# Two of four weight-quarter sums of a Strassen-type up projection: from VectorE to GpSimd

## The chip, the cores and the metric

The kernel runs on one core of one Trainium2 chip. The metric is the device time of one execution in microseconds; the figure given for a kernel is the median of its runs.

## What is computed

One layer of a hybrid encoder on 512 tokens of 2048 channels, all in float32: a normalised input projection, a convolution branch and a neighbourhood attention branch, an output projection, and then the part that matters here, a gated MLP with 5632 hidden units:

```python
xn = rms_norm(x, ffn_norm_g[l])
up = jnp.einsum("bsd,df->bsf", xn, w_up[l])          # 2048 -> 2 * 5632
up = depthwise_conv(up, ffn_dw_w[l], ffn_dw_b[l])    # width 3
gate, val = jnp.split(up, 2, axis=-1)
x = x + jnp.einsum("bsf,fd->bsd", jax.nn.silu(gate) * val, w_down[l])
return rms_norm(x, final_norm_g)
```

## The kernel before

Every matrix is split into a high part (float32 rounded to the format that TensorE multiplies in one pass) and a low part (the rest). A product is then three matmuls, `hi*mh`, `hi*ml` and `lo*mh` (lines 120, 121 and 122). Weights arrive in units of 128 x 1024 float32 (512 KB). A unit is loaded by the SP queue (line 104, tile `raw`), ScalarE copies its high part (line 109, `whi`), VectorE subtracts to get the low part (line 110, `wlo`), and TensorE uses both for 24 matmuls.

All units stand in one list, `plan`, in the order in which TensorE uses them. `weights()` is called ahead of each product and makes units until three beyond the present one exist (`AHEAD = 3`). `whi` and `wlo` have four buffers each, `raw` seven; the sums of weights (`ws`) take theirs from the same seven. A scheduler lays out each engine's instructions in a fixed order at build time, by priority and by its own estimate of when operands are ready; at run time each engine and each queue works through its order strictly.

The up projection goes tile by tile over 44 tiles `f` of 128 hidden units; a tile has a gate half and a value half, and the reduction over 2048 channels is cut in two as well. That makes a 2 x 2 scheme of weight quarters A11, A21, A22, A12, each 128 x 1024, and of token halves of 256 columns, and instead of eight products the kernel makes seven (c = 0 to 6), in the manner of Strassen and Winograd. The factors of the seven products are made by `factors(f)`: three are quarters as they are (c = 0, 3, 5), four are sums:

- c = 1, line 539: `ws = A21 + A22`
- c = 2, line 541: `A21 = A21 + A11`, in place in the tile of A21
- c = 4, line 546: `ws = ws + A11`
- c = 6, line 550: `ws = ws + A12`

Each is one instruction on tiles of 128 x 1024, and `add` is `nc.vector.tensor_add`. The sum then goes through the same two steps as any unit (lines 109 and 110). The results of the seven products (`pu`, three accumulators in turn for c = 0 to 5 and another one for c = 6) are put together on ScalarE and VectorE: the copies `vv` and `uu` (lines 602 and 606) and the adds of lines 605 to 611. Then come the scaling by the norm (627, 628), the convolution (619 on ScalarE, 620 and 621 on VectorE), the Silu (630) and the product with the value half (631).

Four tiles make a group, and there are eleven groups. At the end of a group its four results are split into `hh` (line 636, ScalarE) and `hl` (line 637, VectorE). The down projection of a group runs during the next group, one unit of `w_down` behind the products c = 3 and c = 6 of each tile (line 120 to 122 with `pd`). Its results are copied by ScalarE (line 649, `pdc`) and added to the residual in DRAM by accumulating transfers that GpSimd issues (line 650, `x2d<-pdc`); apart from a few small instructions at the start that is all that GpSimd does. The first group has no down projection beside it, and in the last group the units are spread otherwise. The last group's own down projection comes at the end, with the final norm.

Of the kernel before, what the change touches and what calls it, by code (L numbers as in the profile page):

```python
# [13 lines left out]
ALU = mybir.AluOpType  # L14
# [50 lines left out]
def layer(ctx: ExitStack, tc: tile.TileContext, xT, w_in, w_out, w_up, w_down, par, tab, out):  # L65
    nc = tc.nc
# [19 lines left out]
    def t4(shape, name):  # L86

        return wpool.tile(shape, F32, tag="raw", name=name, bufs=NR)
# [13 lines left out]
    def raw_unit(src, n):  # L102
        raw = t4([P, U * P], "raw")
        return raw, nc.sync.dma_start(raw[:, :n], src)

    def parts(raw, n):
        hi = wpool.tile([P, U * P], F32R, tag="whi", name="whi", bufs=NW)
        lo = wpool.tile([P, U * P], F32R, tag="wlo", name="wlo", bufs=NW)
        i = nc.scalar.activation(hi[:, :n], raw[:, :n], AF.Copy)  # L109
        j = nc.vector.tensor_sub(lo[:, :n], raw[:, :n], hi[:, :n].bitcast(F32))  # L110
        return hi, lo, i, j
# [416 lines left out]
    def factors(f):  # L528

        def load(q):  # L530
            a[q] = raw_unit(w_up[f, q], U * P)[0]
            return a[q]

        def make(c):
            if c == 0:
                return load(A22)
            if c == 1:
                a["s"] = t4([P, U * P], "ws")
                add(a["s"], load(A21), a[A22])
            elif c == 2:  # L540
                add(a[A21], a[A21], load(A11))
                return a[A21]
            elif c == 3:
                return a[A11]
            elif c == 4:
                add(a["s"], a["s"], a[A11])
            elif c == 5:
                return load(A12)
            else:
                add(a["s"], a["s"], a[A12])  # L550
            return a["s"]

        a = {}
        return [lambda c=c: parts(make(c), U * P)[:2] for c in range(7)]

    A11, A21, A22, A12 = range(4)
    add = nc.vector.tensor_add
# [203 lines left out]
```

## Time and profile before

| | us |
|---|---|
| median of 3 runs | 2101.67 |
| lowest and highest run | 2101.33, 2106.94 |
| profiled execution, span from the first to the last instruction | 2106.4 |
| TensorE busy in it | 2067.0 |
| VectorE busy | 1575.8 |
| ScalarE busy | 988.8 |
| GpSimd busy | 140.1 |

The page of the profile gives the span of the profiled execution and no other time of it. In its rows PE is TensorE, PEld its weight loads, DVE VectorE, ACT ScalarE, POOL GpSimd and SP the queue that issues most transfers. A group's row names the line, the engine, the operation, what is written from what, the shapes, the count, then the busy time and the mean of one, and after the bar how long the engine stood idle ahead of these instructions and what ended that. A row of a timeline gives start and length in us, then the instruction, and in brackets the idle time ahead of it and what ended it. A row of waits gives who waited for whom, the total, the number of times and the longest.

### The profile page before, as it was taken

How to read it: one execution, taken by the hardware profiler on the slowest of the kernel's cores; microseconds unless marked ns; L12 is line 12 of the kernel's file. 1: busy time of each engine (PE TensorE's matmuls, PEld its weight loads, DVE VectorE, ACT ScalarE, POOL GpSimd, SP SyncE). 2: the span in 40 equal slices, each digit the busy share in tenths (PEclk: the TensorE clock that was granted, in tenths of full speed). 3: DMA queues.
4: the chain of work that ended last, by engine and by line, in shares of the span. 5: the costliest groups of instructions: out<-in, count | busy, mean ns of one | idle time of the engine just before them, and what ended most of it. 6: DMA issues, size and time to landing. Idle time of an engine off the chain costs nothing.

```text
span 2106.4 us, 32366 instructions
## 1 busy us (share of the span) xinstructions
PE 2067.0 (98%) x13024; PEld 1853.7 (88%) x13024; DVE 1575.8 (75%) x2137; ACT 988.8 (47%) x1472; POOL 140.1 (7%) x166
## 2 busy tenths in 40 slices
PE   8999999999999999999999999999999999999997
PEld 6888888877878899999999999999999999998986
DVE  7986796686568897777777777777776777768666
ACT  6144424456436554454544544454454445444442
POOL 0000000000000001110111101101001011010110
PEclk9999999999999999999999999999999999999998
DMA  6233223236224235565565555556656556553672
GB/s 226 90 121 100 92 89 105 99 108 213 97 96 135 80 121 135 127 138 141 122 142 138 135 136 141 130 131 145 138 127 141 141 131 131 140 135 99 145 203 81
DMA packets 95910, 270.89 MB, mean 129 GB/s; under 512 B 10640, under 2 KB 14736, under 8 KB 95760
## 3 DMA queue, kind: packets, MB, share of 16 engines
q1 hardware_dynamic: 72720, 226.88, 34.4%
q0 software_dynamic: 23040, 41.95, 14.4%
q8 instruction: 102, 1.67, 0.3%
q14 instruction: 48, 0.39, 0.1%
HBM read 218.46 MB, written 50.33 MB: 128 GB/s over the span
## 4 chain that ended last, share of the span: by engine, by line
PE 96%; DVE 2%; DMA 1%; ACT 1%; issue 0%; SPq 0%; DVEq 0%; ACTq 0%
PE pu L120 14%; PE pu L122 14%; PE pu L121 14%; PE pd L122 8%; PE pd L120 8%; PE pd L121 8%; PE pj L120 7%; PE pj L122 7%; PE pj L121 7%; PE po L120 3%; PE po L121 3%; PE po L122 3%; PE sc L366 1%; PE po L409 1%; PE trp L396 1%; DMA raw<-in_w_up 1%
## 5 line engine op out<-in xcount | busy, mean ns | idle before, releaser
L110 DVE TENSOR_TENSOR wlo<-raw,whi 128x1024 fp32r<-128x1024 f32 x368 | 449.3, 1222 | 361.8 <-ACT whi L109 336.6
L120 PE MATMUL pu<-xc,whi 128*128 128x256 f32 x2464 | 699.8, 284 | 8.2 <-ACT vv L602 4.7
L122 PE MATMUL pu<-xc,wlo 128*128 128x256 f32 x2464 | 699.5, 284 | 0.0
L121 PE MATMUL pu<-xc,whi 128*128 128x256 f32 x2464 | 699.5, 284 | 0.0
L109 ACT ACTIVATE whi<-raw 128x1024 fp32r<-128x1024 f32 x368 | 389.2, 1059 | 627.7 <-PE pj L121 217.1
L120 PEld LDWEIGHTS pu<-xc,whi 128*128 128x128 f32 x2464 | 474.5, 193 | 12.8 <-ACT vv L602 4.9
L121 PEld LDWEIGHTS pu<-xc,whi 128*128 128x128 f32 x2464 | 474.6, 193 | 3.5 <-issue 0.4
L122 PEld LDWEIGHTS pu<-xc,wlo 128*128 128x128 f32 x2464 | 474.5, 193 | 0.0
L650 POOL DMA_DIRECT2D x2d<-pdc x160 | 139.4, 873 | 1902.0 <-ACT pdc L649 1794.1
L120 PE MATMUL pj<-xh,whi 128*128 128x512 f32 x640 | 254.0, 398 | 7.7 <-ACT whi L109 7.7
L120 PE MATMUL pd<-hh,whi 128*128 128x512 f32 x640 | 250.3, 391 | 1.9 <-ACT pdc L649 1.9
L122 PE MATMUL pj<-xh,wlo 128*128 128x512 f32 x640 | 250.6, 392 | 0.7 <-DVE wlo L110 0.6
L121 PE MATMUL pj<-xl,whi 128*128 128x512 f32 x640 | 251.2, 393 | 0.0
L121 PE MATMUL pd<-hl,whi 128*128 128x512 f32 x640 | 250.3, 391 | 0.0
L122 PE MATMUL pd<-hh,wlo 128*128 128x512 f32 x640 | 248.9, 391 | 0.0
L109 ACT ACTIVATE whi<-ws 128x1024 fp32r<-128x1024 f32 x132 | 139.9, 1060 | 192.9 <-PE pu L121 135.1
L280 DVE SCALAR_TENSOR_TENSOR y<-ch,prm,y 128x507 f32<-128x507 f32 (+14 forms) x240 | 170.1, 741 | 3.1
L110 DVE TENSOR_TENSOR wlo<-ws,whi 128x1024 fp32r<-128x1024 f32 x132 | 161.3, 1222 | 12.4 <-ACT whi L109 11.8
L649 ACT ACTIVATE pdc<-pd 128x512 f32<-128x512 f32 x160 | 94.0, 588 | 133.4 <-PE pd L122 133.3
L120 PEld LDWEIGHTS pj<-xh,whi 128*128 128x128 f32 x640 | 120.8, 189 | 36.1 <-ACT whi L109 9.0
L122 PEld LDWEIGHTS pj<-xh,wlo 128*128 128x128 f32 x640 | 120.7, 189 | 27.7 <-DVE wlo L110 2.1
L122 PEld LDWEIGHTS pd<-hh,wlo 128*128 128x128 f32 x640 | 120.3, 188 | 28.1 <-DVE wlo L110 3.4
(141 smaller groups left out, 2452.7 us busy)
## 6 DMA issues: line engine op xcount, KB each, us to landing
raw<-in_w_up SPq DMA_DIRECT2D x176, 512.0 KB, 3.5
raw<-in_w_down SPq DMA_DIRECT2D x88, 512.0 KB, 4.0
raw<-in_w_in SPq DMA_DIRECT2D x80, 512.0 KB, 3.7
x2d<-pdc POOLq DMA_DIRECT2D x160, 256.0 KB, 4.7
raw<-in_w_out SPq DMA_DIRECT2D x32, 512.0 KB, 3.4
x<-in_xT SPq DMA_DIRECT2D x32, 256.0 KB, 6.0
tab<-in_tab SPq DMA_DIRECT2D x32, 256.0 KB, 4.0
x2d<-x SPq DMA_DIRECT2D x16, 256.0 KB, 2.0
```

What stands on the lines that cost most here:

```text
L109: i = nc.scalar.activation(hi[:, :n], raw[:, :n], AF.Copy)
L110: j = nc.vector.tensor_sub(lo[:, :n], raw[:, :n], hi[:, :n].bitcast(F32))
L120: nc.tensor.matmul(ps, hi[:, a], mh, start=start, stop=False)
L121: nc.tensor.matmul(ps, hi[:, a], ml, start=False, stop=False)
L122: return nc.tensor.matmul(ps, lo[:, a], mh, start=False, stop=stop)
L280: nc.vector.scalar_tensor_tensor(y[:, a:b], h[:, a + j - PAD:b + j - PAD], prm[:, o + j:o + j + 1], y[:, a:b], op0=ALU.mult, op1=ALU.add)
L366: m = nc.tensor.matmul(both[:, j, i, :], q[hp, b * P:(b + 1) * P], grid(k, KC0[b], KW)[hp], start=True, stop=True)
L396: m = nc.tensor.transpose(ps[:, 2 * i + ch, :], s[:, i, ch * P:(ch + 1) * P], ident)
L409: m = nc.tensor.matmul(grid(po, b * BLK, BLK)[hp], vt[b // 2][:, 2 * (b % 2) + ch, hp], pts[j][:, 2 * i + ch, :], start=(ch == 0), stop=(c ...
L649: nc.scalar.activation(t, ps, AF.Copy)
L650: nc.gpsimd.dma_start(xd[d], t, accum_op=ALU.add)
```

## The change

The sums for c = 1 and c = 2 are issued on GpSimd; those for c = 4 and c = 6 stay on VectorE. Operands, order in the program, tiles and everything else are as before.

```diff
             if c == 1:
                 a["s"] = t4([P, U * P], "ws")
-                add(a["s"], load(A21), a[A22])
+                nc.gpsimd.tensor_tensor(a["s"], load(A21), a[A22], op=ALU.add)
             elif c == 2:
-                add(a[A21], a[A21], load(A11))
+                nc.gpsimd.tensor_tensor(a[A21], a[A21], load(A11), op=ALU.add)
                 return a[A21]
```

## The prediction

> **What bounds the kernel now.** I read the page's first part, then the table of windows, then the waits of TensorE in the gated MLP, and last the rows around each wait. A window row gives the stretch, its length, then busy time and count for PE, PEld, DVE, ACT and POOL, and the granted clock.
>
> ```profile
> PE 2067.0 (98%) x13024; PEld 1853.7 (88%) x13024; DVE 1575.8 (75%) x2137; ACT 988.8 (47%) x1472; POOL 140.1 (7%) x166
> ```
>
> ```profile
> 740.27:760.43 20.16, 20.16 (x170) 20.16 (x169) 20.11 (x25) 10.05 (x13) 0.00 (x0) 1.00 0.33 111
> ...
> 1200.00:1500.00 300.00, 300.00 (x2078) 280.62 (x2078) 221.44 (x260) 142.54 (x188) 33.05 (x38) 1.00 0.59 137
> ```
>
> TensorE is the bound: it is busy for all of the 300 us of the second window at full clock, and nothing that only makes VectorE lighter there can show. VectorE is busy 74% of it. The first window is one tile of hidden units in the first group of four, where no down-projection units are interleaved: there VectorE is busy 20.11 of 20.16 us, so both engines are full at once. The kernel can therefore win only where TensorE waits, and lose wherever VectorE is already just in time. TensorE's waits from the end of the output projection on, and those of its weight loads, are few:
>
> ```profile
> PE pu L120 <- ACT vv L602: 4.7, 1, 4.7
> PE pu L120 <- ACT whi L109: 3.5, 1, 3.5
> ```
>
> ```profile
> PEld pd L122 <- DVE wlo L110: 3.4, 8, 0.4
> ```
>
> The first is one wait of 4.7 us, the second one of 3.5 us at the start of the MLP. The third is the telling one: eight times the weight load of a down product waits up to 0.4 us for VectorE's low half. Eight times VectorE has no slack left at all.
>
> **What moves, and its price.** The two adds of L539 and L541 run 44 times each on VectorE:
>
> ```profile
> L541 DVE TENSOR_TENSOR raw<-raw 128x1024 f32<-128x1024 f32 x44 | 53.7, 1221 | 4.7 <-DMA raw<-in_w_up 4.7
> ...
> L539 DVE TENSOR_TENSOR ws<-raw 128x1024 f32<-128x1024 f32 x44 | 53.6, 1219 | 3.1 <-DMA raw<-in_w_up 3.1
> ```
>
> ```profile
> L650 POOL DMA_DIRECT2D x2d<-pdc x160 | 139.4, 873 | 1902.0 <-ACT pdc L649 1794.1 <-ACT uu L606 95.2 <-DMA raw<-in_w_down 12.7
> masks.py:199 POOL TENSOR_SCALAR_AFFINE_SELECT ident<-ident 128x128 f32<-128x128 f32 x1 | 0.3, 287 | 0.1
> masks.py:197 POOL MEMSET ident<- 128x128 f32 x1 | 0.2, 204 | 0.3 <-POOLq L753 0.3
> L753 POOL MEMSET const-bfloat16-1.0<- 128x1 bf16 x1 | 0.1, 101 | 0.0
> ```
>
> The rows around one of them, in the timelines of VectorE and GpSimd at a boundary between two groups:
>
> ```profile
> 911.76 1.23 DVE L110 TENSOR_TENSOR wlo<-raw,whi 128x1024 fp32r<-128x1024 f32 x1 [3.56 <-ACT whi L109]
> 912.95 0.75 DVE L620 SCALAR_TENSOR_TENSOR uy<-g,prm,uy 128x511 f32<-128x511 f32 x1
> 913.62 1.22 DVE L539 TENSOR_TENSOR ws<-raw 128x1024 f32<-128x1024 f32 x1
> 914.75 0.75 DVE L621 SCALAR_TENSOR_TENSOR uy<-g,prm,uy 128x511 f32<-128x511 f32 x1
> ...
> 919.14 1.22 DVE L110 TENSOR_TENSOR wlo<-raw,whi 128x1024 fp32r<-128x1024 f32 x1
> ```
>
> ```profile
> 912.62 0.87 POOL L650 DMA_DIRECT2D x2d<-pdc  x1 [2.58 <-ACT pdc L649]
> ```
>
> One add lasts 1.22 us on VectorE and holds its queue for 1.13 us (913.62 to 914.75). On GpSimd no add is shown. The nearest rows: 128 columns written take 204 ns and one column 101, so a written column is 0.81 ns; one input more makes it 287 ns, so a column read is about 0.65 ns. An add of 1024 columns that reads two inputs and writes one is estimated at 0.1 + 1024 x (0.81 + 2 x 0.65) ns = 2.26, say 2.3 us. The bounds are VectorE's own 1.22 us below, and above twice a one-input pass, 2 x (0.1 + 1024 x 1.46 ns) = 3.2 us. GpSimd's total becomes 140 + 88 x 2.3 = 342 us, far from full. Its queue is in order: an add may stand behind an issue of L650 that waits for the copy of a down product, and an issue behind an add that waits for a load. I cost both at nothing, because the row of L650 shows that the engine idles 1902 us, and because no instruction but the final loads of x reads what L650 sends. If an add did come up one issue late, that is 0.87 us on a sum made up to three products ahead of its use, 3 x 2.88 us (a product is a seventh of the 20.16 us of the first window).
>
> The disputed price is what an add on GpSimd does to VectorE beside it. Let x be the time that VectorE loses to one add. Before, x is 1.13. Either the engines don't disturb each other, and x is 0; or VectorE's instructions, nearly all of which read two tiles from the same memory, stand still while the add runs, and x is its 2.3 us (up to 3.2). No row decides: the issue of 912.62 runs beside L110 and L620, which keep their 1.23 and 0.75 us, but an issue reads no tile. I take x = 2.3, since the nearest instruction, an add of the same three tiles on VectorE, takes its turn among the others whole; 0 and 3.2 stay as ends. The page "SBUF — State Buffer" of the Trainium skill (Who interferes with whom) says that a VectorE instruction with two SBUF inputs contends with a GpSimd instruction that reads SBUF, and that the second to start waits for all of the first. By that rule x is a whole add and the sum below comes to 2110.5 us, by the issue rows alone x is 0 and it comes to 2094.3; no row here shows the one or the other.
>
> *The eight group boundaries.* Of the boundary above, TensorE's rows:
>
> ```profile
> 919.80 0.39 PE L120 MATMUL pd<-hh,whi 128*128 128x512 f32 x1
> 920.03 0.40 PE L121 MATMUL pd<-hl,whi 128*128 128x512 f32 x1
> 920.42 0.50 PE L122 MATMUL pd<-hh,wlo 128*128 128x512 f32 x1
> ```
>
> From 911.76 VectorE runs without a gap to the low half of 919.14, which ends at 920.36; the L122 of TensorE follows at 920.42 instead of 920.26 (products of 512 columns come every 0.23 us, as from 919.80 to 920.03). GpSimd is free at 913.5 and the tile is loaded, since L539 ran at 913.62 without waiting. So the add falls inside this run in both cases. With x = 2.3 the low half ends 2.3 - 1.13 = 1.17 us later and TensorE waits that much more: 8 x 1.17 = +9.4 us. With x = 0 the existing wait goes: 8 x 0.16 = -1.3 us at least, -3.4 by the waits row.
>
> *The first group.*
>
> ```profile
> 719.78 1.22 DVE L539 TENSOR_TENSOR ws<-raw 128x1024 f32<-128x1024 f32 x1
> ...
> 758.53 1.23 DVE L110 TENSOR_TENSOR wlo<-ws,whi 128x1024 fp32r<-128x1024 f32 x1
> ...
> 777.08 1.23 DVE L541 TENSOR_TENSOR raw<-raw 128x1024 f32<-128x1024 f32 x1
> ```
>
> ```profile
> 763.55 0.28 PE L122 MATMUL pu<-xc,wlo 128*128 128x256 f32 x1
> ```
>
> Six moved adds lie in the stretch where VectorE is full, from the first to the last shown. They would put it 6 x 1.17 = 7.0 us behind. The slack: the low half of 758.53 is done at 759.76 and first used at 763.55 (the last product of that tile), 3.8 us. What is left over, 7.0 - 3.8 = +3.2 us, is TensorE's. With x = 0 it is nothing, since TensorE doesn't wait there.
>
> *The start of the MLP.*
>
> ```profile
> 702.04 1.22 DVE L541 TENSOR_TENSOR raw<-raw 128x1024 f32<-128x1024 f32 x1
> ```
>
> ```profile
> 709.28 1.22 DVE L550 TENSOR_TENSOR ws<-ws,raw 128x1024 f32<-128x1024 f32 x1
> ```
>
> VectorE works from 702.04 through the operands of the first products and the norm's small steps to L550, which the 3.5 us wait follows through ScalarE. L541 stands in this chain: +1.2 us with x = 2.3, -1.1 with x = 0.
>
> *The last group's boundary.* Here the move takes away a wait.
>
> ```profile
> 1913.20 1.22 DVE L541 TENSOR_TENSOR raw<-raw 128x1024 f32<-128x1024 f32 x1 [4.38 <-DMA raw<-in_w_up]
> ```
>
> ```profile
> 1917.64 0.63 ACT L630 ACTIVATE uy<-uy 128x512 f32<-128x512 f32 x1 [5.64 <-DVE uy L621]
> ...
> 1920.68 0.63 ACT L602 ACTIVATE vv<-pu 128x256 f32<-128x256 f32 x2
> ```
>
> ```profile
> 1921.09 0.56 PE L120 MATMUL pu<-xc,whi 128*128 128x256 f32 x1 [4.70 <-ACT vv L602]
> ```
>
> ```profile
> 1911.00:1928.00 17.00, 12.30 (x90) 12.10 (x90) 14.21 (x17) 6.95 (x12) 0.00 (x0) 0.90 0.35 95
> ```
>
> L541 holds VectorE's queue for 4.38 us for a load that is not needed yet; the convolution behind it is late, so ScalarE's Silu, so the copy that frees TensorE's accumulator: 4.7 us of wait, and 1.7 us more because the granted clock is 0.90 over these 17 us. On GpSimd the same wait holds only GpSimd's queue. The convolution moves up by 4.38 + 1.13 us, more than the wait; next late is nothing within it. Ends: 0, if the new order of instructions puts another wait there, to -6.4. I take -5, because the span of 2106.4 us lies 4.7 us above the median of the runs, so that the median may hold less of such stalls.
>
> **The sum.** The page gives the span, 2106.4 us, and no other time of that execution; the median of the runs is 2101.67 (2101.33 to 2106.94), and I add the change to the median. With x = 2.3: +9.4 + 3.2 + 1.2 - 5 = +8.8, so **2110.5 us**.
>
> **Rivals.** *Undisturbed engines (faster).* x = 0: -5 - 1.3 - 1.1 = -7.4, so 2094.3; with the longer ends -6.4 - 3.4 - 1.1, 2090.8. For it: GpSimd's issues leave VectorE's 1.22 us as it is. Against it: none of them reads a tile. It decides below x = 1.0, where 9 x (x - 1.13) - 5 passes -6.3.
>
> *The two effects cancel (no change).* Between x = 1.0 and x = 2.13 the sum 9 (x - 1.13) + what 6 (x - 1.13) exceeds 3.8 by - 5 stays within 6.3 us of nothing; in the middle, x = 1.6, it is -0.8, so 2100.9. For it: GpSimd may have to wait for gaps, and VectorE's instructions from the accumulators need not stop. Against it: the boundary run has no gap and hardly such an instruction.
>
> *A longer add (slower still).* At 3.2 us each (x - 1.13 = 2.07) the boundaries cost 16.6, the first group 12.4 - 3.8 = 8.6, the start 2.1; less 5, 2124. For it: GpSimd's steps are shown only at 128 columns. Against it: the estimate from three rows gives 2.3.
>
> **How the numbers follow.** 0.3%, 6.3 us, is about what a measurement of this kernel can tell from no change. VectorE stopped for the whole add has 0.42, of which 0.06 is the longer add; cancelling 0.26; undisturbed 0.32. The first is the likeliest, so 2110.5. Its own range is 2107 to 2122. The range for all takes in the undisturbed case near its end and the longer add nearly whole: 2091 to 2122. Faster 0.32, same 0.26, slower 0.42.
>
> **What would show it.** Right: L110 and L620/L621 on VectorE get means above 1.22 and 0.75 us, or VectorE shows gaps beside L539/L541; the row "PEld pd L122 <- DVE wlo L110" grows from 0.4 to about 1.6 us each, eight times; POOL gets 88 adds near 2.3 us; the 4.7 us wait on L602 is gone. Wrong: VectorE's means stay and the eight waits vanish (undisturbed), a new wait of TensorE on "whi" filled from a sum (adds too late), or the wait on L602 stays with another releaser behind it.

## The result, and the profile after

The changed kernel is slower: a median of 2116.89 us in four runs (2115.49 to 2121.64) against 2104.31 for the kernel before in four runs (2101.33 to 2108.62). The ratio is 1.0069 with an interval of 1.0056 to 1.0082, which is 14.5 us (11.8 to 17.3); the medians by themselves lie 12.6 us apart. The profiled execution of after has a span of 2113.7 us and a time of 2115.49, the lowest of its four.

The engines' totals, from the first part of the page of after:

```profile
PE 2068.2 (98%) x13024; PEld 1853.2 (88%) x13024; DVE 1659.1 (78%) x2049; ACT 982.4 (46%) x1472; POOL 363.5 (17%) x254
```

VectorE (DVE) lost 88 adds of 1.22 us, 107 us of work, and is busy 83.3 us longer than before (1575.8). What is left on it must have grown by some 190 us, about 2.2 us for each add that now runs on GpSimd. The groups of instructions show where, GpSimd's first, then VectorE's (after the bar: busy us, mean ns of one):

```profile
L539 POOL TENSOR_TENSOR ws<-raw 128x1024 f32<-128x1024 f32 x44 | 122.6, 2786 | 747.9 <-DVE wlo L110 684.9 <-DMA raw<-in_w_up 35.2 <-DVE g L610 20.7
L541 POOL TENSOR_TENSOR raw<-raw 128x1024 f32<-128x1024 f32 x44 | 111.3, 2530 | 303.3 <-DMA raw<-in_w_up 303.3
...
L110 DVE TENSOR_TENSOR wlo<-raw,whi 128x1024 fp32r<-128x1024 f32 x368 | 510.1, 1387 | 283.7 <-ACT whi L109 258.3 <-PE trp L396 13.5 <-PE trv L354 10.0
...
L620 DVE SCALAR_TENSOR_TENSOR uy<-vl,fwn,uy 128x511 f32<-128x511 f32 x44 | 108.9, 2474 | 0.0
L550 DVE TENSOR_TENSOR ws<-ws,raw 128x1024 f32<-128x1024 f32 x44 | 70.6, 1604 | 1.0
...
L605 DVE TENSOR_TENSOR vl<-vv,pu 128x512 f32<-128x512 f32 x44 | 29.8, 678 | 0.0
```

One step of the convolution, L620 on the value half, takes 2.47 us in the mean where the prediction's boundary rows have 0.75; L110 and L550 grow as well. L605, which reads one tile from memory and one from TensorE's accumulators, doesn't grow and holds nothing up either: by the timelines seven of its 44 instructions begin behind the start of an add and take 0.67 us in the mean, and the 30 adds that begin while it runs take 2.40 us in the median.

The boundary between two groups that the prediction worked out, in the timelines of GpSimd, VectorE and TensorE:

```profile
918.12 2.78 POOL L539 TENSOR_TENSOR ws<-raw 128x1024 f32<-128x1024 f32 x1
929.11 2.39 POOL L541 TENSOR_TENSOR raw<-raw 128x1024 f32<-128x1024 f32 x1 [8.21 <-DMA raw<-in_w_up]
```

```profile
916.69 1.23 DVE L110 TENSOR_TENSOR wlo<-raw,whi 128x1024 fp32r<-128x1024 f32 x1 [3.51 <-ACT whi L109]
917.88 0.75 DVE L620 SCALAR_TENSOR_TENSOR uy<-g,prm,uy 128x511 f32<-128x511 f32 x1
918.59 2.86 DVE L620 SCALAR_TENSOR_TENSOR uy<-vl,fwn,uy 128x511 f32<-128x511 f32 x1
...
922.69 0.68 DVE L637 TENSOR_TENSOR hl<-uy,hh 128x512 fp32r<-128x512 f32 x1
...
923.89 0.68 DVE L637 TENSOR_TENSOR hl<-uy,hh 128x512 fp32r<-128x512 f32 x1
924.50 1.21 DVE L110 TENSOR_TENSOR wlo<-raw,whi 128x1024 fp32r<-128x1024 f32 x1
...
929.11 0.67 DVE L605 TENSOR_TENSOR vl<-vv,pu 128x512 f32<-128x512 f32 x1
929.70 2.88 DVE L550 TENSOR_TENSOR ws<-ws,raw 128x1024 f32<-128x1024 f32 x1
```

```profile
924.26 0.40 PE L120 MATMUL pd<-hh,whi 128*128 128x512 f32 x1
924.49 0.40 PE L121 MATMUL pd<-hl,whi 128*128 128x512 f32 x1
925.76 0.50 PE L122 MATMUL pd<-hh,wlo 128*128 128x512 f32 x1 [0.87 <-DVE wlo L110]
```

The add of 918.12 comes up while VectorE is in its first L620 and ends at 920.90. The second L620 is issued at 918.59 and ends at 921.45, 0.55 us after the add: it takes 2.86 us, 2.11 more than its own 0.75, so it has stood still for nearly all of the add. The low half of 924.50 ends at 925.71, and TensorE, which could have used it at 924.72, takes it at 925.76. Eleven us on, the add of 929.11 starts beside L605, which ends on time; L550 behind it ends at 932.58, 1.08 us after the add, as if it had begun there. The add itself takes 2.39 us; the 0.39 more of the first one is its own wait for VectorE.

TensorE's waits in after, then those of its weight loads:

```profile
PE pd L122 <- DVE wlo L110: 8.8, 9, 1.8
...
PE pu L120 <- ACT xc L490: 2.1, 1, 2.1
...
PE pu L120 <- ACT whi L109: 1.0, 1, 1.0
...
PE pd L121 <- DVE hl L637: 0.7, 1, 0.7
...
PE pu L120 <- ACT vv L602: 0.7, 1, 0.7
```

```profile
PEld pd L122 <- DVE wlo L110: 12.6, 9, 2.2
```

The eight waits of up to 0.4 us became nine that cost TensorE 8.8 us: 1.8 at the first boundary, about 0.87 at each of the next eight. The wait of 4.7 us on L602 is 0.7. The 3.5 us at the start of the MLP are 2.1 and 1.0. Below are two windows: the prediction's second one, and the one of its last group, which lies 3.4 us behind the group's first product and so begins at 1922.97 here:

```profile
1200.00:1500.00 300.00, 298.24 (x2074) 279.26 (x2073) 240.68 (x237) 142.80 (x193) 83.17 (x59) 1.00 0.53 133
1922.97:1939.97 17.00, 16.34 (x136) 16.14 (x136) 16.38 (x20) 9.19 (x14) 3.50 (x2) 1.00 0.49 136
```

In the first, TensorE is idle 1.76 us, two boundaries of 0.87; VectorE does 23 instructions fewer and is busy 19 us longer. In the second, TensorE is busy for 16.34 of the 17 us at a granted clock of 1.00, where before it had 12.30 at 0.90. For the sum by stages I count in each trace where the first product of a group starts (us; the last column is the end of the span):

| kernel | group 0 | 1 | 2 | 10 | end | mean length of groups 2 to 9 |
|---|---|---|---|---|---|---|
| before | 698.22 | 786.35 | 910.70 | 1907.60 | 2106.4 | 124.61 |
| after | 698.20 | 788.21 | 915.63 | 1919.57 | 2113.7 | 125.49 |

Counted in the same way, the first five tiles of the MLP (the four of group 0 and the first of group 1, with the first boundary in it) take 27.65, 20.16, 20.16, 20.16 and 31.11 us before, and 27.11, 20.16, 20.93, 21.81 and 34.18 us after.

### The profile page after: what moved, and what is told of

Read it like the earlier page. It is cut to its first block, busy times and chain, and to the rows that moved or that the text cites. A ratio compares the mean times of both kernels' runs of the same rounds, so it can differ in the third digit from the quotient of the medians.

```text
span 2113.7 us, 32580 instructions
## 1 busy us (share of the span) xinstructions
PE 2068.2 (98%) x13024; PEld 1853.2 (88%) x13024; DVE 1659.1 (78%) x2049; ACT 982.4 (46%) x1472; POOL 363.5 (17%) x254
## 4 chain that ended last, share of the span: by engine, by line
PE 89%; DVE 8%; issue 2%; ACT 1%; DMA 1%; SPq 0%; DVEq 0%; ACTq 0%
PE pu L120 12%; PE pu L121 12%; PE pu L122 12%; PE pd L122 8%; PE pd L120 8%; PE pd L121 7%; PE pj L120 7%; PE pj L122 7%; PE pj L121 7%; PE po L120 3%; PE po L121 3%; PE po L122 3%; DVE wlo L110 2%; DVE uy L620 2%; DVE uy L621 1%
## 5 line engine op out<-in xcount | busy, mean ns | idle before, releaser
L110 DVE TENSOR_TENSOR wlo<-raw,whi 128x1024 fp32r<-128x1024 f32 x368 | 510.1, 1387 | 283.7 <-ACT whi L109 258.3
L539 POOL TENSOR_TENSOR ws<-raw 128x1024 f32<-128x1024 f32 x44 | 122.6, 2786 | 747.9 <-DVE wlo L110 684.9
L110 DVE TENSOR_TENSOR wlo<-ws,whi 128x1024 fp32r<-128x1024 f32 x132 | 167.6, 1270 | 23.5 <-ACT whi L109 18.7
L541 POOL TENSOR_TENSOR raw<-raw 128x1024 f32<-128x1024 f32 x44 | 111.3, 2530 | 303.3 <-DMA raw<-in_w_up 303.3
L122 PEld LDWEIGHTS pd<-hh,wlo 128*128 128x128 f32 x640 | 120.6, 188 | 38.1 <-DVE wlo L110 12.6
```

Source lines behind the costliest of these rows:

```text
L122: return nc.tensor.matmul(ps, lo[:, a], mh, start=False, stop=stop)
L539: nc.gpsimd.tensor_tensor(a["s"], load(A21), a[A22], op=ALU.add)
L541: nc.gpsimd.tensor_tensor(a[A21], a[A21], load(A11), op=ALU.add)
```

## The experiments

Ten kernels ran. Line numbers shift by a few in them; the rows below say which instruction is meant.

**The kernel before, once more.** It shows how much of a profiled execution is chance.

> The kernel before, unchanged, once more. Theory A (the last group's wait is there in some executions only): the profiled span is near 2099.7 us and the 4.7 us wait of TensorE on L602 near 1916 is gone or under 1 us; then the change was worth 14 us against such an execution, and 7 us against the one profiled first. Theory B (the wait belongs to the order of instructions and is always there): the wait is 4 to 5 us again whatever the span. Under both the ratio is 1.000 within 0.3%.

It took 2103.88 against 2103.17 us, ratio 1.0004 (0.9995 to 1.0012). TensorE's wait in its profile:

```profile
PE pu L120 <- ACT vv L602: 1.4, 1, 1.4
```

The same program, and the 4.7 us of the last group are 1.4: not under the 1 us of theory A, whose span of 2099.7 us became 2103.7, and not the 4 to 5 us of theory B. From the first product of the last group to the end it took 195.0 us, where the first profile has 198.8. Most of that stall belongs to one execution, in which a load came late: the sum of L541 that waits for it starts 5.60 us behind the group's first product in the first profile and 2.26 us in this one.

**One sum at a time.** First only c = 1, then only c = 2:

```diff
-                add(a["s"], load(A21), a[A22])
+                nc.gpsimd.tensor_tensor(a["s"], load(A21), a[A22], op=ALU.add)
```

> Only the sum of c = 1 (L539) on GpSimd, that of c = 2 stays on VectorE. Theory of place (an add stops a two-input instruction of VectorE for about 2 us, and that costs only where VectorE is just in time): L539 is the one that lies in the eight group boundaries, so these waits stay near 1 us each, and about half of the first group's loss remains: +8 to +11 us. Theory of count (each add on GpSimd costs a like share): half of 14.5, +7 us. Theory of late sums: waits of TensorE on whi, none on wlo.

```diff
-                add(a[A21], a[A21], load(A11))
+                nc.gpsimd.tensor_tensor(a[A21], a[A21], load(A11), op=ALU.add)
```

> Only the sum of c = 2 (L541) on GpSimd. Theory of place: L541 runs behind the low half that the boundary needs, so the eight waits return to about 0.3 us each; in the first group three adds instead of six, lag 3 us at most, within the slack: 0 to +3 us, and the wait of 4.38 us of VectorE on a load in the last group is gone, so up to -6 in executions that have it. Theory of count: +7 us.

Against 2103.17 us, c = 1 alone took 2117.26 us, ratio 1.0059 (1.0045 to 1.0074), and c = 2 alone 2111.28, ratio 1.0032 (1.0019 to 1.0044). TensorE's waits, of c = 1 alone and then of c = 2 alone:

```profile
PE pd L122 <- DVE wlo L110: 8.8, 9, 1.8
```

```profile
PE pd L122 <- DVE wlo L110: 1.8, 1, 1.8
```

The nine boundary waits belong to c = 1, digit for digit as in after; groups 2 to 9 are 125.49 us long with c = 1 alone and 124.62 with c = 2 alone, as before. By their times both kernels missed the theory of place: 12.4 us by the ratio for c = 1, above its +8 to +11, and 6.7 for c = 2, above its 0 to +3 and at the +7 of the theory of count. Where the time goes decides against the count: c = 2 costs nothing in groups 2 to 9, 1.8 us in the last three tiles of the first group, where VectorE is full, and 4.5 us in the tile behind them, whose wait of 1.8 us is the only one of its kind. That tile has the first boundary, which the theory of place had left out: VectorE comes to it without its lead. The two losses don't add up to that of after, because each contains this boundary and after contains it once: against before the tile is 6.1 us longer with c = 1 alone, 4.5 with c = 2 alone and 3.1 in after. TensorE waits there for 3.1, 2.5 and 2.5 us. The rest goes with the granted clock, which is 0.91 over the 37.2 us of this tile with c = 1 alone, 0.95 over 35.6 us with c = 2 alone, and 1.00 in after; by these figures it is worth an estimated 3.3 and 1.8 us. Why it fell in two of the three profiles, no run shows.

**Adds anywhere but at the tight places.** Both sums go to GpSimd in 29 tiles, those from the seventh on (`f > 5`) but for the second tile of each group, whose sums stand in the boundary run:

```diff
+        def gadd(o, x, y):
+            if f > 5 and f % 4 != 1:
+                nc.gpsimd.tensor_tensor(o, x, y, op=ALU.add)
+            else:
+                add(o, x, y)
...
-                add(a["s"], load(A21), a[A22])
+                gadd(a["s"], load(A21), a[A22])
...
-                add(a[A21], a[A21], load(A11))
+                gadd(a[A21], a[A21], load(A11))
```

> Both sums on GpSimd, but only for tiles f above 5 that are not the second of a group: 58 of the 88 adds; those in the first group and those that fall into a group boundary stay on VectorE. Theory of place: VectorE still loses about 2 us to each of the 58, but TensorE's eight waits are back at about 0.3 us: 0 to +2 us. Theory of count: 58/88 of 14.5, +9.6 us.

It took 2102.58 against 2103.17 us, ratio 0.9996 (0.9985 to 1.0006): 58 adds on GpSimd for nothing. Its groups of VectorE (L626 is L620 of before), its weight loads' waits and its window:

```profile
L110 DVE TENSOR_TENSOR wlo<-ws,whi 128x1024 fp32r<-128x1024 f32 x132 | 218.2, 1653 | 13.8 <-ACT whi L109 13.2
L626 DVE SCALAR_TENSOR_TENSOR uy<-vl,fwn,uy 128x511 f32<-128x511 f32 x44 | 92.0, 2090 | 0.0
```

```profile
PEld pd L122 <- DVE wlo L110: 3.4, 8, 0.4
```

```profile
1200.00:1500.00 300.00, 300.00 (x2082) 280.80 (x2082) 238.62 (x246) 142.74 (x190) 76.26 (x53) 1.00 0.58 137
```

VectorE is held as much as in after, 238.62 us busy in the window against 221.44 before, with 76.26 us of GpSimd beside it. TensorE is busy for all 300 us. Being held costs nothing where VectorE is ahead.

**Only the boundary adds.** The reverse: nine adds, c = 1 of the second tile of each group from the third on.

```diff
-                add(a["s"], load(A21), a[A22])
+                load(A21)
+                if f > 5 and f % CH == 1:
+                    nc.gpsimd.tensor_tensor(a["s"], a[A21], a[A22], op=ALU.add)
+                else:
+                    add(a["s"], a[A21], a[A22])
```

> Only nine of the 88 adds on GpSimd: the sum of c = 1 of the second tile of each group from the third group on (f = 9, 13 to 41), which fall into the group boundaries; the other 79 stay on VectorE. Theory of place: the eight waits grow from 0.3 to about 1.2 us, +0.87 us each, +7 us with a tenth of the adds. Theory of count: 9/88 of 14.5, +1.5 us.

It took 2112.31 against 2102.31 us, ratio 1.0044 (1.0032 to 1.0057): 9.2 us from nine adds, where 58 others cost none. GpSimd's group and TensorE's waits:

```profile
L541 POOL TENSOR_TENSOR ws<-raw 128x1024 f32<-128x1024 f32 x9 | 24.7, 2740 | 3.5 <-DMA raw<-in_w_up 3.5
```

```profile
PE pd L122 <- DVE wlo L110: 7.0, 8, 0.9
...
PE pu L120 <- ACT vv L606: 3.1, 1, 3.1
```

Eight waits of 0.87 us, 7.0 in all, and nothing else new but the wait of the last group (L606 is L602), which is 1.4 or 4.7 in executions of the kernel before. The interval, 6.7 to 12.0 us, takes in the 7.0; what the 9.2 hold beyond it is not placed.

**What GpSimd does beside VectorE.** In two kernels the sums stay on VectorE and GpSimd gets other work 44 times on tiles of the same size: first a `memset` of the tile of A11 ahead of its load, which writes and reads nothing; then a copy of A11 onto itself after the load, which reads one tile and writes one.

```diff
-            a[q] = raw_unit(w_up[f, q], U * P)[0]
+            a[q] = t4([P, U * P], "raw")
+            if q == A11:
+                nc.gpsimd.memset(a[q], 0.0)
+            nc.sync.dma_start(a[q], w_up[f, q])
```

> All four sums on VectorE; GpSimd only writes: it fills the tile of A11 with zeros ahead of its load (44 times 128x1024, the load waits for it). If GpSimd's reading stops VectorE, the two-input instructions beside the fill keep their 1.22 and 0.75 us. If any GpSimd instruction of that size does, those beside it grow by up to the fill's length, about 0.9 us. The time itself is not the point: the loads of A11 come about 1 us later.

```diff
-                add(a[A21], a[A21], load(A11))
+                load(A11)
+                nc.gpsimd.tensor_copy(a[A11], a[A11])
+                add(a[A21], a[A21], a[A11])
```

> All four sums on VectorE; GpSimd copies A11 in place after its load (44 times 128x1024, one input, one output), ahead of the sum of c = 2. If GpSimd's reading stops VectorE, two-input instructions beside the copy grow by about its length (estimated 1.6 us from the 287 ns row), and those with an accumulator as second input (L605, 0.68 us) don't. If only a two-input GpSimd instruction does it, nothing grows. Theory of place: the time grows by 0 to 8 us, as with L541 alone.

The `memset` kernel took 2104.71 us in its one run, against a median of 2105.02. Its group on GpSimd, and L620 of before (L623 here) on VectorE:

```profile
L533 POOL MEMSET raw<- 128x1024 f32 x44 | 42.0, 954 | 987.5 <-DVE wlo L110 931.7 <-ACT whi L109 55.9
...
L623 DVE SCALAR_TENSOR_TENSOR uy<-vl,fwn,uy 128x511 f32<-128x511 f32 x44 | 32.8, 745 | 0.0
```

Writing alone disturbs nothing: all 44 take 0.95 or 0.96 us and VectorE keeps its times. The copy kernel took 2109.54 us in one run, inside the runs of the kernel before beside it (2100.21 to 2111.23), so its time decides nothing. Its timelines of GpSimd and VectorE do (L552 is L550 and L622 is L620 of before):

```profile
751.96 1.06 POOL L542 COPY raw<-raw 128x1024 f32<-128x1024 f32 x1 [20.26 <-DMA raw<-in_w_up]
...
1203.63 2.54 POOL L542 COPY raw<-raw 128x1024 f32<-128x1024 f32 x1 [7.44 <-DMA raw<-in_w_up]
```

```profile
752.03 1.53 DVE L622 SCALAR_TENSOR_TENSOR uy<-vl,fwn,uy 128x511 f32<-128x511 f32 x1
...
1202.91 1.22 DVE L552 TENSOR_TENSOR ws<-ws,raw 128x1024 f32<-128x1024 f32 x1
1204.05 1.22 DVE L110 TENSOR_TENSOR wlo<-raw,whi 128x1024 fp32r<-128x1024 f32 x1
```

At 751.96 the copy is in first: it takes 1.06 us (the shortest of the 44 take 1.04), and L622 behind it takes 1.53 instead of 0.75. So one input read on GpSimd is enough to hold VectorE; five of VectorE's instructions in the MLP are held in this way. Issued in the middle of an add of VectorE, at 1203.63, the copy takes 2.54: it waits for that add and for the L110 behind it, and VectorE loses nothing. That is the common case. The expectation, that VectorE's instructions beside the copies grow, came true for these few alone. So both can be held, and who is in first goes on. The page "SBUF — State Buffer" of the Trainium skill (Who interferes with whom) says that a VectorE instruction with two SBUF inputs contends with GpSimd's reads, not with an instruction that only writes, that one with at most one SBUF input does not contend outside the two-port modes, and that the later one blocks fully. The rows agree: 2.86 us instead of 0.75 for L620 beside an add, 0.745 beside a `memset`, 0.67 for L605, with one input from the accumulators, behind the start of an add. That the waiting copy let a second instruction of VectorE pass is more than the page says.

**All four sums on GpSimd.** If what counts is the number of adds, groups 2 to 9 must lose twice as much; if the place, the same.

```diff
+    def gadd(o, x, y):
+        nc.gpsimd.tensor_tensor(o, x, y, op=ALU.add)
...
-                add(a["s"], load(A21), a[A22])
+                gadd(a["s"], load(A21), a[A22])
...
-                add(a[A21], a[A21], load(A11))
+                gadd(a[A21], a[A21], load(A11))
...
-                add(a["s"], a["s"], a[A11])
+                gadd(a["s"], a["s"], a[A11])
...
-                add(a["s"], a["s"], a[A12])
+                gadd(a["s"], a["s"], a[A12])
```

> All four sums on GpSimd (176 adds). Theory of place: VectorE loses about 2 us per add; the eight boundaries keep about 1 us each, and the first group, where VectorE was full, gets 16 adds: VectorE there goes from 20.1 to about 23.7 us per tile of 20.16, so 3.5 us per tile more than fits, 10 to 14 us in all; in the other groups 22.9 - 4.5 + 8.2 = 26.6 of 31.1 us still fits. Together +18 to +26 us. Theory of count: twice 14.5, +29 us. Theory of late sums: waits of TensorE on whi at every tile, since the sums of c = 4 and c = 6 are used soon after they are made.

It took 2134.76 against 2105.02 us, ratio 1.014 (1.0122 to 1.0158), 29.5 us: more than the +18 to +26 of the theory of place and just the +29 of the theory of count. Where it was lost decides once more. Its window, TensorE's waits, and a row of GpSimd in the last group (L560 is `gadd`):

```profile
1200.00:1500.00 300.00, 298.25 (x2074) 279.27 (x2074) 240.08 (x221) 141.75 (x190) 134.11 (x77) 1.00 0.57 137
```

```profile
PE pu L120 <- ACT whi L109: 9.2, 2, 8.1
PE pd L122 <- DVE wlo L110: 8.9, 9, 1.8
```

```profile
1937.32 7.13 POOL L560 TENSOR_TENSOR raw<-raw 128x1024 f32<-128x1024 f32 x1 [4.98 <-DMA raw<-in_w_up]
```

In the middle groups 51 us more of GpSimd's adds cost TensorE nothing: 298.25 us busy against 298.24 in after, and again nine waits of 8.9 us. The first group takes 96.6 us, 8.2 more than the mean of 88.4 in the seven traces in which GpSimd reads no tile there, so less than the 10 to 14 of the expectation. The rest came where I hadn't priced it: group 1 takes 132.8 us (127.4 in after, 124.4 before), and in the last group a product waits 8.1 us for an operand made from a sum on GpSimd. That sum (c = 4) stands in GpSimd's queue behind the add of 1937.32, which takes 7.13 us instead of 2.39, beside a run of VectorE's instructions, from 1936.90 to 1942.27, that all keep their usual times. Here GpSimd is the one that is held.

**Taking the adds out of the boundary run without GpSimd.** In a first attempt both sums stayed on VectorE with a priority 300 steps later.

```diff
-                add(a["s"], load(A21), a[A22])
+                load(A21)
+                with shifted(300):
+                    add(a["s"], a[A21], a[A22])
...
-                add(a[A21], a[A21], load(A11))
+                load(A11)
+                with shifted(300):
+                    add(a[A21], a[A21], a[A11])
```

> All four sums on VectorE; those of c = 1 and c = 2 get a lower priority in the scheduler (300 later), so that they stand behind the instructions that are needed sooner, and the first of them leaves the run ahead of the boundary's low half. Theory of place: the eight waits of 0.3 us go or shrink, and L541 no longer holds VectorE's queue in the last group: 0 to -5 us against before, most likely -2.

2105.54 against 2105.02 us, ratio 1.0003 (0.9991 to 1.0014). VectorE's timeline at the boundary and the weight loads' waits (L541 is the sum of c = 1):

```profile
914.36 1.22 DVE L541 TENSOR_TENSOR ws<-raw 128x1024 f32<-128x1024 f32 x1
```

```profile
PEld pd L122 <- DVE wlo L110: 3.4, 8, 0.4
```

The add stayed in the run, so this says nothing on the question. In the second attempt the two sums of the second tile of a group are issued behind the last L637 of the group before:

```diff
-                add(a["s"], load(A21), a[A22])
+                load(A21)
+                held(f, lambda: add(a["s"], a[A21], a[A22]))
...
-                add(a[A21], a[A21], load(A11))
+                load(A11)
+                held(f, lambda: add(a[A21], a[A21], a[A11]))
...
+    ends = []
+
+    def held(f, do):
+        if ends and f % CH == 1:
+            with tc.issue_after(ends[-1].ins):
+                do()
+        else:
+            do()
...
-        nc.vector.tensor_sub(l, g, h.bitcast(F32))
+        ends.append(nc.vector.tensor_sub(l, g, h.bitcast(F32)))
```

> All four sums on VectorE; those of c = 1 and c = 2 of the second tile of each group are issued behind the last low half of the results of the group before (L637), so that the run ahead of the boundary's low half is one add shorter. Theory of place: the low half comes 1.13 us sooner, the eight waits of TensorE (0.16 us and the slower product behind, 0.3 us each) go, -2 us; in the last group VectorE no longer waits there for a load, so up to 1 us more in a usual execution: -2 to -4 us. If the waits come from something else than the add in front, no change.

2101.15 against 2102.31 us, ratio 0.9992 (0.998 to 1.0003): no difference that can be told. The boundary in its timelines of VectorE and TensorE:

```profile
916.16 1.22 DVE L110 TENSOR_TENSOR wlo<-raw,whi 128x1024 fp32r<-128x1024 f32 x1
```

```profile
918.04 0.40 PE L120 MATMUL pd<-hh,whi 128*128 128x512 f32 x1
918.27 0.40 PE L121 MATMUL pd<-hl,whi 128*128 128x512 f32 x1
918.51 0.39 PE L122 MATMUL pd<-hh,wlo 128*128 128x512 f32 x1
```

The low half is done at 917.38, 1.13 us before its use, and the waits on it are gone; a group takes 124.51 us instead of 124.62. This is after's boundary with the add neither on VectorE in the run nor on GpSimd, and it gives the plainest sum for the loss: hold VectorE there for 2.11 us, and 2.11 - 1.13 = 0.98 us are TensorE's. After's groups are 125.49 - 124.51 = 0.98 us longer than these. All of the loss at these eight boundaries is the held VectorE.

## Why the prediction was right or wrong

- **VectorE is held for the add** (x = 2.3): right, shown by the stretched L620, by the `memset` that holds nothing, and by nine adds that cost 9.2 us. It measures 2.11 at the boundary; the add is 2.39 us alone, where three small rows gave 2.3. The rival of undisturbed engines fell with these rows; that of a longer add fell with the 2.39. Cancelling fell too: with x = 2.11 the prediction's own sum is 8.8 + 2.1 - 5 = +5.9, still within the 6.3 us of no change, but the gain that was to cancel the loss wasn't there.
- **The eight boundaries**: +9.4 forecast, 8 x 0.87 = +7.0 measured. The mechanism and the place were right. The size fitted partly by luck: I kept the order of instructions and only swapped 1.13 for x. VectorE's timeline of the kernel before has three L637 ahead of the low half of 919.14:

```profile
916.08 0.69 DVE L637 TENSOR_TENSOR hl<-uy,hh 128x512 fp32r<-128x512 f32 x1
...
917.34 0.69 DVE L637 TENSOR_TENSOR hl<-uy,hh 128x512 fp32r<-128x512 f32 x1
...
918.54 0.69 DVE L637 TENSOR_TENSOR hl<-uy,hh 128x512 fp32r<-128x512 f32 x1
```

  In after there are two (922.69 and 923.89), 0.60 us less ahead of it; and TensorE uses that half after one pair of products (924.26 and 924.49) where it made two before, 0.47 us sooner. With x - 1.13 = 0.98 that is 0.98 - 0.60 + 0.47 = 0.85, near the 0.87.
- **The first group**: +3.2 forecast. The three tiles of the stretch take 20.16, 20.93 and 21.81 us, where each takes 20.16 in all seven traces in which the first group's sums are on VectorE and GpSimd reads no tile there (before, its repetition, the two kernels with 58 and 9 adds, the `memset`, the two without GpSimd): +2.4. With x = 2.11 the step's own sum, 6 x 0.98 - 3.8, gives 2.1. But the boundary at its end, which I had left out as it isn't among the eight waits, costs 3.1 more (group 1 takes 127.42 instead of 124.35 us), as VectorE comes to it without its lead. Together 5.5: the right stretch and mechanism, its end missed.
- **The start of the MLP**: +1.2 forecast. The chain does come later: L550 starts at 710.29 us instead of 709.28, and the product behind the wait at 712.84 instead of 711.71. But none of it is left at the end of the tile, which takes 27.11 us instead of 27.65, so -0.5. TensorE waits for 2.1 and 1.0 us there instead of 3.5, and the granted clock, 0.94 in the mean of the tile in both, is low at different places: after has 0.88 up to that product and 1.00 in it, before 1.00 and then 0.68. In the seven traces this tile takes 26.13 to 28.55 us, at clocks from 1.00 to 0.88, so one profile of each kernel can't tell a term of this size.
- **The last group's boundary**: this step failed. The 4.7 us did go, in after as forecast, but I took -5 off the sum for a stall that one profile showed. In four profiles with the last group's sums where they were (before, its repetition, the `memset` and the later priority) it takes 198.8, 195.0, 194.9 and 192.5 us, 195.3 in the mean; after's takes 194.1. By these the step is worth -1.2; but the four lie 6.3 us apart and after's is one profile, so what is shown is that a usual execution has no 5 us there to gain. I had the warning in hand, a span 4.7 us above the median, and used it only to round -6.4 down.
- **Sums that come late**: costed at nothing, right for two sums (no such wait in after), wrong for four (8.1 us).
- **The sum**: by these terms -0.5 + 2.4 + 3.1 + 7.0 - 1.2 = +10.8 for the profiled execution of after, which lies 1.4 us under its median: 12.2, beside 12.6 between the medians and 14.5 by the ratio. The forecast of +8.8 was short by the last group's stall (3.8) and the first boundary (3.1); the eight boundaries, the first group and the start, each put too high, hid 4.9 of that, so its nearness is partly luck. The 2 us or so up to the ratio are not placed: after's other three runs have no profile. Of the 6.4 us between 2110.5 and the measured 2116.89, 2.6 are the median of before, which is 2104.31 with a fourth run.

## What to carry to other kernels

Before moving an elementwise operation with two tile inputs to GpSimd, count it as a hold on VectorE for nearly its whole length there (2.4 us instead of 1.2 for 128 x 1024 float32), unless VectorE's work beside it reads only one tile from memory, and look where it will fall: beside a VectorE that is ahead it is free, and in a run where VectorE is just in time it costs more than it saved. Nine instructions out of 88 made most of this loss. And a single long wait in one profile should be looked for in a second profile of the same kernel before it is booked as a gain.

## What the runs showed of the hardware that was not expected

- Who holds whom depends on who is in first. The adds of c = 1 mostly come up inside L620's pair (36 of 44) and hold VectorE for 2.1 us; the one-input copies (1.04 us at the shortest) are mostly issued inside an add of VectorE and wait themselves, with a mean of 2.05 us, and 24 of the 44 let the next VectorE instruction pass as well. With all four sums on GpSimd one add stood for 4.7 us beside a whole run of VectorE's instructions. What lets an add in between two instructions of VectorE and keeps a copy out is left open by these runs.
- A change of engine for two lines altered the order of instructions on VectorE and TensorE at the eight boundaries; that moved the time of the first use by 0.47 us, about half of the 0.88 us that each of them lost.
